# A two-layer hybrid decoder step: projections as seven block products for all tokens at once, with results passed through DRAM

## The chip, the cores and the metric

The kernel runs on one core of one Trainium2 chip. The metric is the device time of one execution in microseconds (us). The kernel before took 1739.54 to 1741.24 us in three runs, with a median of 1740.52 us. A profile of one more execution comes with it. In the profile PE is TensorE (PEld its weight loads), DVE is VectorE, ACT is ScalarE, POOL is GpSimd, and SP is SyncE, which issues all of this kernel's DMAs in one queue, in order.

## The reference, cut to what matters

One inference step of a decoder with two layers: 1024 prompt tokens, and 8 sample tokens (one each for 8 sequences with their own caches). The model is 1024 wide.

```python
for i in range(DEPTH):                      # 2
    hp, hs = rmsnorm(xp, norm_g[i]), rmsnorm(xs, norm_g[i])
    if i % 2 == 0:   # sliding-window attention, window 128, 32 heads of 64, 4 KV heads
        q, k, v, g = split(h @ w_in_attn)   # widths 2048, 256, 256, 2048
        o = softmax(q k^T / 8 + bias, masked, with a sink per head) v
    else:            # retention, 4 heads, 256 for q and k, 512 for v, chunks of 128
        q, k, v, g = split(h @ w_in_ret)    # widths 1024, 1024, 2048, 2048
        q, k = rotary(q), rotary(k) / 16
        o = groupnorm((q k^T * decay) v + (q R) * cross)
        R = gamma**128 * R + k_dec^T v
    x = x + (silu(g) * o) @ w_out           # 2048 x 1024
return rmsnorm(x), caches and states
```

All of it is float32. The largest part are the input projections: 4608 output features in layer 0 and 6144 in layer 1, each with an inner dimension of 1024, for 1032 tokens.

## The kernel before, in words

**A product in float32.** Every large operand is split in two: a high part rounded to fp32r (`whi`, `hh`, `yh`) and the rest (`wlo`, `hl`, `yl`). A product is three matmuls into one PSUM bank: high by high, high by low, low by high (lines 359 to 361). For a weight tile of 128x512 the split is one cast on ACT (line 175) and one subtraction, by turns on POOL and DVE (line 179).

**Two halves of the tokens.** The tokens are worked on in halves: half A is 512 prompt tokens and the 8 samples (520 columns, cut in 260 and 260), half B the other 512. The activations stand transposed, with features on the partitions. Each half goes through all weights of a layer, so each weight tile is loaded and split once for each half.

**The stream.** `Stream` holds the projection jobs in order. A job that produces 128 output features takes two weight tiles and 24 matmuls for each column block (`proj_job`), and evacuates the block from PSUM straight into what comes next: queries to their high and low parts (`q_jobs`), gates through silu (`g_jobs`, `rg_jobs`), rotary (`rot_jobs`). Values are made with the tokens on the PSUM partitions (`tok_job`). PSUM has four single banks for such jobs (`gps`, line 121). Output projections are jobs as well (`out_job`, `out1_job`): eight for each group of 512 inner features; each adds its product into the resident x.

**The order.** The order on PE is the order of the program text, written by hand; that of the other engines is planned from a model of their times. `spread(n, stages)` puts small pieces of attention or retention between n jobs of the stream. In layer 0 there are 64 attention pieces (two halves, eight groups of four heads, four blocks of 128 queries), each with scores (line 624), a softmax (lines 590 to 602), transposes (line 641) and values (line 663). In layer 1 there are 32 retention chunks (`ret_scores`, `ret_values`, `ret_turn`), and for each head one `ret_sample`, which reads and writes the sample states.

**Norms.** The norm of the next half or layer (`norm_stats`, `norm`) runs between attention pieces. In the first 30 us the input is taken in (`first_x`), in the projections' own order; its norm factor is applied after the product.

## Time and profile before

| | before |
|---|---|
| three runs, us | 1739.54, 1740.52, 1741.24 |
| profiled execution, its time and its span, us | 1736.38; 1734.6 |
| PE busy; PEld busy | 1697.7 us (98%); 1450.0 us (84%) |
| DVE; ACT; POOL busy | 60%; 48%; 41% of the span |
| DMA | 211.31 MB, 39.5% of 16 engines' time |
| mean granted TensorE clock | 0.994 |

The span is the time from the first to the last instruction. A matmul's shown duration contains the depth of its pipeline, and so the durations of matmuls that follow each other overlap: what one costs is read from the distance between two starts in the timeline, not from its duration. Groups of instructions are given by line, engine and operation, with tile names (out<-in), shape and count. The chain of waits is the sequence of work that ended last.

### The profile page before, as it was taken

Reading aid. Unit: us, or ns where it says so; the run is one execution under the profiler, and the core shown is the slowest. Engines: PE = TensorE matmul, PEld = TensorE weight load, DVE = VectorE, ACT = ScalarE, POOL = GpSimd, SP = SyncE. Lnnn points to the kernel's source line nnn. Section 1 sums busy time; section 2 is a strip of 40 time slices with the busy share of each in tenths; the row PEclk is TensorE's granted clock in tenths of the full one; section 3 lists DMA queues with packets and bytes.
Section 4 is the critical chain, followed back from the end, with each engine's and each line's share of the span. In section 5 each row is a group of like instructions: output and inputs, shape, how many; then the busy total and the mean of one; then the engine's idle time right before and its main releaser. Section 6 shows DMA issues by size and latency. Waiting matters only on the chain.

```text
span 1734.6 us, 29003 instructions
## 1 busy us (share of the span) xinstructions
PE 1697.7 (98%) x10550; PEld 1450.0 (84%) x10550; DVE 1045.5 (60%) x2142; ACT 841.1 (48%) x1960; POOL 713.2 (41%) x670
## 2 busy tenths in 40 slices
PE   9999999999999999999999999999999999999997
PEld 8989999988887777779788797897777889888887
DVE  6777676784576565773475545566555655445366
ACT  5566465555556464654344444344343433433344
POOL 3244344353344343444334235344353353433534
PEclk9999999999999999999999999999999999999998
DMA  5523333333253323223476445466463262322323
GB/s 153 142 62 91 123 105 104 89 108 91 85 172 90 85 75 92 80 86 106 120 244 192 143 152 188 128 195 206 129 217 111 85 194 73 98 86 81 102 69 121
DMA packets 124174, 211.31 MB, mean 122 GB/s; under 512 B 17128, under 2 KB 28000, under 8 KB 124032
## 3 DMA queue, kind: packets, MB, share of 16 engines
q1 hardware_dynamic: 124032, 209.47, 39.5%
q8 instruction: 83, 1.36, 0.3%
q14 instruction: 59, 0.48, 0.1%
HBM read 177.57 MB, written 33.91 MB: 122 GB/s over the span
## 4 chain that ended last, share of the span: by engine, by line
PE 81%; DVE 5%; DMA 3%; ACT 2%; POOL 2%; issue 1%; SPq 0%; POOLq 0%; ACTq 0%; DVEq 0%
PE gemm L359 12%; PE gemm L360 12%; PE gemm L361 12%; PE gemm L386 4%; PE gemm L387 3%; PE gemm L388 3%; PE o L663 3%; PE gemm L1063 3%; PE gemm L1062 3%; PE gemm L1064 3%; PE gemm L414 3%; PE gemm L416 3%; PE gemm L415 3%; PE S L624 3%; PE pt L641 1%
## 5 line engine op out<-in xcount | busy, mean ns | idle before, releaser
L179 POOL TENSOR_TENSOR wlo<-wraw,whi 128x512 fp32r<-128x512 f32 x236 | 311.7, 1321 | 555.6 <-ACT whi L175 524.0
L359 PE MATMUL gemm<-hh,whi 128*128 128x260 f32 (+1 forms) x1584 | 520.9, 329 | 0.0
L361 PE MATMUL gemm<-hh,wlo 128*128 128x260 f32 (+1 forms) x1584 | 506.2, 320 | 0.4 <-POOL wlo L179 0.4
L360 PE MATMUL gemm<-hl,whi 128*128 128x260 f32 (+1 forms) x1584 | 506.2, 320 | 0.0
L175 ACT CAST whi<-wraw 128x512 fp32r<-128x512 f32 x472 | 290.5, 617 | 442.9 <-PE gemm L360 136.5
L359 PEld LDWEIGHTS gemm<-hh,whi 128*128 128x128 f32 x1584 | 298.2, 188 | 45.0 <-issue 15.3
L361 PEld LDWEIGHTS gemm<-hh,wlo 128*128 128x128 f32 x1584 | 298.0, 188 | 23.3 <-POOL wlo L179 0.6
L360 PEld LDWEIGHTS gemm<-hl,whi 128*128 128x128 f32 x1584 | 298.5, 188 | 20.2 <-issue 0.5
L179 DVE TENSOR_TENSOR wlo<-wraw,whi 128x512 fp32r<-128x512 f32 x236 | 190.1, 806 | 161.6 <-ACT whi L175 159.5
L431 POOL TENSOR_TENSOR yl<-yf,yh 128x256 fp32r<-128x256 f32 x128 | 107.3, 847 | 96.7 <-ACT yh L430 96.3
L414 PE MATMUL gemm<-yh,whi 128*128 128x260 f32 (+1 forms) x384 | 126.9, 330 | 4.4 <-DVE xa L418 4.4
L386 PE MATMUL gemm<-whi,hh 128*128 128x512 f32 (+1 forms) x320 | 123.1, 385 | 2.9 <-DVE ra L748 2.8
L598 ACT ACTIVATE L<-L,nm 128x128 f32<-128x128 f32 x256 | 99.8, 391 | 52.2 <-DVE nm L593 51.8
L1062 PE MATMUL gemm<-yh,whi 128*128 128x260 f32 (+3 forms) x384 | 124.7, 325 | 0.0
L416 PE MATMUL gemm<-yh,wlo 128*128 128x260 f32 (+1 forms) x384 | 123.2, 321 | 0.0
L415 PE MATMUL gemm<-yl,whi 128*128 128x260 f32 (+1 forms) x384 | 123.0, 320 | 0.0
L1063 PE MATMUL gemm<-yl,whi 128*128 128x260 f32 (+3 forms) x384 | 122.8, 320 | 0.0
L1064 PE MATMUL gemm<-yh,wlo 128*128 128x260 f32 (+3 forms) x384 | 122.8, 320 | 0.0
L388 PE MATMUL gemm<-whi,hl 128*128 128x512 f32 (+1 forms) x320 | 120.0, 375 | 2.0 <-DVE hl L1099 1.8
L387 PE MATMUL gemm<-wlo,hh 128*128 128x512 f32 (+1 forms) x320 | 120.4, 376 | 0.0
L602 POOL TENSOR_TENSOR L<-L,rsum 128x512 f32<-128x512 f32 x64 | 76.4, 1193 | 79.3 <-DVE rsum L601 45.4
L414 PEld LDWEIGHTS gemm<-yh,whi 128*128 128x128 f32 x384 | 72.6, 189 | 15.2 <-ACT whi L175 4.8
(246 smaller groups left out, 3141.8 us busy)
## 6 DMA issues: line engine op xcount, KB each, us to landing
wraw<-in_w_in SPq DMA_DIRECT2D x264, 256.0 KB
wraw<-in_w_out SPq DMA_DIRECT2D x136, 256.0 KB
wraw<-in_w_v SPq DMA_DIRECT2D x72, 256.0 KB
Rsm<-in_state SPq DMA_DIRECT2D x64, 256.0 KB
out_ret_state_sample<-Rsm SPq DMA_DIRECT2D x64, 256.0 KB
vrow<-vdram SPq DMA_DIRECT2D x32, 256.0 KB
bias<-bdram SPq DMA_DIRECT2D x16, 256.0 KB
xdram<-xa SPq DMA_DIRECT2D x16, 256.0 KB
```

The lines of the kernel that those rows point to most:

```text
L175: act.copy(hi, raw)
L179: eng.tensor_tensor(out=lo, in0=raw, in1=r32(hi), op=ALU.subtract)
L359: pe.matmul(ps, a, hh[k][:, c0:c1], start=(k == 0), stop=False)
L360: pe.matmul(ps, a, hl[k][:, c0:c1], start=False, stop=False)
L361: pe.matmul(ps, b, hh[k][:, c0:c1], start=False, stop=(k == KT - 1))
L386: pe.matmul(ps, hh[k][:, cs], wh, start=(k == 0), stop=False)
L414: pe.matmul(ps, a, yh[:, k % 2, c0:c1], start=(k == 0), stop=False)
L415: pe.matmul(ps, a, yl[:, k % 2, c0:c1], start=False, stop=False)
L416: pe.matmul(ps, b, yh[:, k % 2, c0:c1], start=False, stop=(k == 3))
L1062: pe.matmul(ps, a, yh[:, k % 2, c0:c1], start=(k == 0), stop=False)
L1063: pe.matmul(ps, a, yl[:, k % 2, c0:c1], start=False, stop=False)
L1064: pe.matmul(ps, b, yh[:, k % 2, c0:c1], start=False, stop=(k == 3))
```

## The change

**Seven products a unit.** A unit is a pair of feature tiles (2 x 128 output features), the inner dimension in two halves of 512, and for each half of the tokens two blocks of columns: 256, and 256 with the samples (264; zeros stand in for the samples in half B). Plainly these are eight block products. The kernel after makes seven, with sums and differences of blocks (the form that is known as Winograd's): four weight blocks a, c, b, d give seven weight tiles (`mixed`), the four blocks of activations seven mixtures (`mixtures`). Each product is 12 matmuls (four inner tiles, three parts) for each half of the tokens; both halves are served from the same weight tile, `hi, lo`. Three results are put together outside PSUM. The seven mixtures of both halves, each with a high and a low part, stay in SBUF throughout a layer.

**Values** of both layers are made by such units as well, features on the partitions, and turned on PE afterwards (`v_unit`'s `turn`, `ret_scores`).

**PSUM.** A unit has two tiles of two banks (`a` and `y`); the next unit begins with their roles exchanged.

**Through DRAM.** Results of q, k, g and of all of layer 1 are stored (`spill`, or the end of `rot_unit`), and read back where they are needed (`load_gq`, `load_k`, `ret_load`); so are the gated branch outputs (`ydram`, `load_y`). Queries and keys are no longer split: scores are plain float32 with an inner dimension of 64, the two heads of a pair on partitions 0 to 63 and 64 to 127, their results in different banks.

**Output projections** come after the units as a stage of their own, with x read from DRAM and written back for every group of 512 inner features (`x_from`, `x_to`), both halves to one weight tile. Each x, each loaded branch output and each pair of rotary tables take one of three buffers (`flat`).

**Order.** In layer 0: values and keys of half A alone, of half B alone, 16 units of q and g with attention in between from the third on, then the output stage. In layer 1: gates of the first head for each half alone, the other units with retention between, the output stage.

```diff
-AHEAD = 2
+AHEAD = 1
+DEEP = 3
...
     def fetch(self, n):
         while self.todo and len(self.ready) < n:
-            self.ready.append(self.load(self.todo.pop(0)))
+            for w in self.todo[: 1 + DEEP]:
+                w.load()
+            self.ready.append(self.todo.pop(0).prep())
...
+    def big(name, dt=F32):
...
+        return ap_.tile([P, 2, 2 * QS], dt, name=name, tag="b", bufs=NBIG)
...
+    NBIG = 6
+    NHF = 3
...
+    def flat(name):
+        return ap_.tile([P, 2 * QS], F32, name=name, tag="hf", bufs=NHF)
...
+    def wtile():
+        return wp.tile([P, 512], F32, name="wraw", tag="wr", bufs=5)
...
+    def mixed(wa, wb):
...
+        def third():
+            minus(d["a"], d["b"], d["a"], vec)
+            d["t"] = wtile()
+            return wsplit(minus(d["t"], d["d"], d["a"], vec), vec)
...
+        return [
+            Weights(get(a=wa[0]), lambda: wsplit(d["a"], pool)),
+            Weights(get(c=wa[1]), lambda: wsplit(d["c"], pool)),
+            Weights(get(b=wb[0], d=wb[1]), third),
+            Weights(None, lambda: wsplit(d["a"], pool)),
+            Weights(None, lambda: wsplit(minus(d["b"], d["d"], d["b"], pool), vec)),
+            Weights(None, lambda: wsplit(d["d"], pool)),
+            Weights(None, lambda: wsplit(minus(d["c"], d["c"], d["t"], pool), vec)),
+        ]
...
+    def part(h, c, k, src, eng):
...
+        act.copy(hh, src)
+        eng.tensor_tensor(out=hl, in0=src, in1=r32(hh), op=ALU.subtract)
...
+    def mixtures(h, k, f):
...
+        a1, a2 = f[:, 0, 0:QS], f[:, 0, QS : 2 * QS]
+        b1, b2 = f[:, 1, 0:QT], f[:, 1, QS : 2 * QS]
+        part(h, 0, k, a1, pool)
+        part(h, 1, k, b1, vec)
+        part(h, 6, k, b2, vec)
+        vec.tensor_tensor(out=b2, in0=a2, in1=b2, op=ALU.add)
+        pool.tensor_tensor(out=a2, in0=a1, in1=a2, op=ALU.subtract)
+        vec.tensor_tensor(out=a1, in0=b2, in1=a1, op=ALU.subtract)
+        part(h, 2, k, a1, vec)
+        part(h, 3, k, b2, pool)
+        part(h, 4, k, a2, vec)
+        vec.tensor_tensor(out=b1, in0=b1, in1=a1[:, 0:QT], op=ALU.subtract)
+        part(h, 5, k, b1, pool)
...
+    def unit_job(wa, wb, done, halves=(0, 1)):
...
+            def product(ps, c, n, first):
+                hi, lo = stream.tile()
+                for i in range(nh):
+                    o = ps[:, i, :n]
+                    for k in range(4):
+                        hh, hl = [x[:, :n] for x in hcs[i][c][k]]
+                        wh, wl = hi[:, k * P : (k + 1) * P], lo[:, k * P : (k + 1) * P]
+                        pe.matmul(o, wh, hh, start=(first and k == 0), stop=False, skip_group_check=not first)
+                        pe.matmul(o, wh, hl, start=False, stop=False, skip_group_check=not first)
+                        pe.matmul(o, wl, hh, start=False, stop=(k == 3), skip_group_check=not first)
...
+            t = product(a, 0, QS, True)
+            x00 = ctile(0, nh)
+            act.copy(x00, aq)
+            yield t
+            t = product(y, 1, QT, True)
+            plus(x00, yq)
+            done(0, 0, x00, False)
+            yield t
+            t = product(a, 2, QS, False)
+            x10 = ctile(0, nh)
+            act.copy(x10, aq)
+            yield t
+            t = product(y, 3, QS, True)
+            x11 = ctile(1, nh)
+            act.copy(x11, yw)
+            yield t
+            t = product(a, 4, QS, False)
+            plus(x11, aw)
+            yield t
+            t = product(y, 5, QT, False)
+            plus(x10, yq)
+            done(1, 0, x10, False)
+            done(1, 1, x11, False)
+            yield t
+            t = product(a, 6, QS, False)
+            done(0, 1, aw, True)
+            yield t
...
+        for j in range(2):
+            for par in range(2):
+                r = slice(64 * par, 64 * par + 64)
+                pe.matmul(S[:, 2 * par + j, w0:256], q[r, j, cs], kk[r, (gb - 1) * P + w0 : (gb + 1) * P], start=True, stop=True)
...
+    def load_y(l, u):
...
+                f = flat("yf")[:, :T]
+                sp.dma_start(f, ydram[l][u][:, kt, h, 0:T])
...
+                act.copy(yh, f)
+                (pool if kt % 2 else vec).tensor_tensor(out=yl, in0=f, in1=r32(yh), op=ALU.subtract)
...
+    def rot_unit(f0, dr):
...
+            a = ctile(q, 2)
+            vec.tensor_tensor(out=a, in0=x1, in1=sin, op=ALU.mult)
...
+            vec.tensor_tensor(out=sin, in0=sin, in1=x2, op=ALU.mult)
+            pool.tensor_tensor(out=x2, in0=x2, in1=cos, op=ALU.mult)
+            vec.tensor_tensor(out=o1, in0=o1, in1=sin, op=ALU.subtract)
+            pool.tensor_tensor(out=x2, in0=x2, in1=a, op=ALU.add)
...
+    spread(outs[4], [stager(norm(0))] * 6)
+    spread(2, [stager(norm(1))] * 6)
+    stream.finish(2)
```

More of the change, by code (lines that the diff above doesn't have):

```diff
@@ L222, in norm_stats, with final_part @@
+    XF = {}
+    def final_part(c0, c1):
+        w = c1 - c0
+        xs = [XF[1, kt][:, c0:c1] for kt in range(KT)]
         s = None
         for kt in range(KT):
[L224 to L234 removed]
@@ L285, in final_part @@
[L285 to L291 removed]
+            b = flat("sqb")[:, :w]
             act.activation(b, xs[kt], AF.Square)
@@ L775, in rk_jobs @@
[L775 to L798 removed]
+    RS, RQ = {}, {}
```

1273 lines of the change are left out of this document (607 added, 666 removed).

## The prediction, made before the result was known

> **What bounds the kernel now.** I read the page's busy times and the chain of waits first, then the timeline of PE, then the grouped instructions.
>
> ```profile
> span 1734.6 us, 29003 instructions
> PE 1697.7 (98%) x10550; PEld 1450.0 (84%) x10550; DVE 1045.5 (60%) x2142; ACT 841.1 (48%) x1960; POOL 713.2 (41%) x670
> q1 hardware_dynamic: 124032, 209.47, 39.5%
> PE 81%; DVE 5%; DMA 3%; ACT 2%; POOL 2%; issue 1%; SPq 0%; POOLq 0%; ACTq 0%; DVEq 0%
> ```
>
> PE is the bound: 81% of the chain runs on it, and no other engine comes near its span. So PE's work counts first, and then every place where PE would begin to wait. A matmul's price is the distance between starts:
>
> ```profile
> 199.81 0.28 PE L359 MATMUL gemm<-hh,whi 128*128 128x260 f32 x1
> ...
> 202.57 0.28 PE L361 MATMUL gemm<-hh,wlo 128*128 128x260 f32 x1
> ...
> 999.77 0.40 PE L1062 MATMUL gemm<-yh,whi 128*128 128x512 f32 x1
> ...
> 1002.33 0.40 PE L1064 MATMUL gemm<-yh,wlo 128*128 128x512 f32 x1
> ...
> 1705.52 0.28 PE L1064 MATMUL gemm<-yh,wlo 128*128 128x256 f32 x1
> ...
> 1707.32 0.28 PE L1064 MATMUL gemm<-yh,wlo 128*128 128x256 f32 x1
> 1707.43 0.29 PE L1062 MATMUL gemm<-yh,whi 128*128 128x264 f32 x1
> ...
> 1710.26 0.28 PE L1064 MATMUL gemm<-yh,wlo 128*128 128x264 f32 x1
> ```
>
> The first and last of 24, 12, 16 and 24 in a row give 2.76/23 = 0.120 us for 260 columns, 2.56/11 = 0.233 for 512, 1.80/15 = 0.120 for 256, 2.83/23 = 0.123 for 264. The price follows the columns; cutting 512 in two costs nothing that shows, so the weight loads behind do not bind at these widths.
>
> **Products removed and added.** The counts of before:
>
> ```profile
> L359 PE MATMUL gemm<-hh,whi 128*128 128x260 f32 x1056 | 308.0, 292 | 0.0
> L359 PE MATMUL gemm<-hh,whi 128*128 128x512 f32 x528 | 212.9, 403 | 0.0
> L386 PE MATMUL gemm<-whi,hh 128*128 128x512 f32 x256 | 103.5, 404 | 2.9 <-DVE ra L748 2.8
> L386 PE MATMUL gemm<-whi,hh 128*128 128x256 f32 x64 | 19.6, 307 | 0.0
> L391 PE MATMUL vsp<-wlo,hs 128*40 128x512 f32 x32 | 12.6, 394 | 0.0
> ```
>
> Lines 360, 361, 387 and 388 have the same counts as 359 and 386, line 390 those of 391. Removed: 3168 x 0.120 + (1584 + 768 + 64) x 0.233 + 192 x 0.120 = 380 + 563 + 23, with some 2 us for 16 narrow sample products 968 us. Added: layer 0 has 18 units' worth (values and keys split by halves), layer 1 has 24. Each is 5 products of 24 matmuls at 264 columns and 2 at 256: 120 x 0.123 + 48 x 0.120 = 20.5 us. 42 units are 862 us. PE saves **106 us**, 11% instead of one eighth because of the zero columns. The output projections have as many columns as before.
>
> **PE work that comes in.** Scores change from eight split matmuls to four plain ones with an inner dimension of 64; values and their weights of attention are as they were.
>
> ```profile
> 202.69 0.60 PE L641 MATMUL pt<-cst,L 128*128 128x128 f32 x4
> 203.05 0.37 PE L359 MATMUL gemm<-hh,whi 128*128 128x260 f32 x1
> 226.60 1.01 PE o L663 x8
> 219.64 0.96 PE S L624 x8
> 307.67 1.10 PE rps L211 x2
> ```
>
> A plain matmul shows as two records, and `rps`, one of 512 columns, takes 1.10 us: 4 x 0.233 and the pipeline's depth, so four passes. Eight records of `o` are four plain matmuls of 256 columns; one after the other they would take 16 x 0.120 = 1.9 us. They take 1.01 us: two column halves of the array run side by side. For two row halves no row stands here: from 0.96 us (side by side, no change) to 1.9 us, or 0 to +61 us over 64 pieces. I take 0 by the row of `o`, nearest in kind, and add 0.25 us of a change of mode on either side, 16 us in all (before and after the eight records of `o` the neighbours stand so much further apart than 0.120). Turning values on PE: 128 + 18 transposes more, at 0.36/4 = 0.09 us, with the samples' small ones 15 us. Together **+31 us**.
>
> In a sentence that the sum doesn't use: the Trainium skill, TensorEngine Tiling (Array Packing), Gotcha 1: PSUM Pressure, says that row tiles can't reach the same PSUM bank at once; the code sends the two heads' scores to different banks, so that by it too the 61 us would stay away, and without that placing they would be paid; no run here shows it.
>
> **Work on the other engines.** Prices:
>
> ```profile
> L179 POOL TENSOR_TENSOR wlo<-wraw,whi 128x512 fp32r<-128x512 f32 x236 | 311.7, 1321 | 555.6 <-ACT whi L175 524.0
> L179 DVE TENSOR_TENSOR wlo<-wraw,whi 128x512 fp32r<-128x512 f32 x236 | 190.1, 806 | 161.6 <-ACT whi L175 159.5
> L175 ACT CAST whi<-wraw 128x512 fp32r<-128x512 f32 x472 | 290.5, 617 | 442.9 <-PE gemm L360 136.5 <-issue 85.0 <-PE gemm L388 58.5
> L1066 DVE TENSOR_TENSOR xa<-xa,gemm 128x512 f32<-128x512 f32 x32 | 21.9, 684 | 16.9 <-PE gemm L1064 16.5
> L647 ACT COPY ptp<-pt 128x512 f32<-128x512 f32 x56 | 32.3, 577 | 23.7 <-DVE ptc L643 19.9 <-DVE nm L593 3.6
> L558 DVE TENSOR_TENSOR qe<-qf,qe 64x260 fp32r<-64x260 f32 x32 | 16.6, 518 | 7.2 <-ACT qe L557 6.0
> L749 POOL TENSOR_TENSOR rf<-rf,ra 128x512 f32<-128x512 f32 x16 | 23.5, 1492 | 12.1 <-DVE ra L748 12.0
> 50.00:350.00 300.00, 292.10 (x2440) 272.77 (x2439) 216.52 (x506) 173.17 (x501) 122.94 (x121) 1.00 0.35 99
> ```
>
> A unit's weights take 7 casts on ACT (4.3 us), 5 DVE operations (4.0) and 6 on POOL (7.9); its results 4 copies on ACT (2.3) and 3 additions on DVE (2.1). That is 6.6, 6.1 and 7.9 us beside 20.5 us of PE, before attention. DVE is busy 72% from 50 to 350 us, with as many attention pieces to a us of PE as after; I expect the same share there, and no engine becomes the bound over a whole stage. So I cost this at nothing in the middle of the stages. Its cover is one product, 24 x 0.123 = 2.95 us, in which each PSUM tile must be emptied; where the cover is short it is a rival below.
>
> **Where PE waits anew.** The *head*: each of the four pairs of x blocks of a half needs four subtractions and three sums of 264 columns on DVE (7 x 0.52), two scalings and two sums of squares of 528 columns (4 x 0.7 by line 1066), 6.4 us; the first unit needs the last pair. Before, PE's first product came at 6.25 us:
>
> ```profile
> 6.25 0.56 PE L386 MATMUL gemm<-whi,hh 128*128 128x256 f32 x1
> 6.25:24.00 17.75, 15.39 (x108) 14.41 (x107) 16.42 (x33) 11.15 (x20) 8.73 (x6) 0.90 0.53 181
> 257.67 2.61 DMA sqb<-in_x
> 1184.51 4.94 DMA hf<-xdram
> 366.96 0.36 PE L414 MATMUL gemm<-yh,whi 128*128 128x260 f32 x1 [2.95 <-DVE xa L418]
> ```
>
> Now half A's mixtures end at 7 + 26 = 33 us (the first x lands near 7) and half B's, with the weights of the first two units between (2 x 5), near 70; values and keys of half B, 20.5 us, follow: 90 us, where the PE content is 6 + 41 + 2 = 49. That is up to 40 us; if ACT and POOL take their part in time and the scalings run at half, 15. I take +22, as before lost some 8 here itself. The *layer change* has the same work without squares (two halves, 5 us a pair, 20 us each) beside 22 us of output products and 20 us of gates: between +5 and +30, I take +12. In the eight *half-size units* 1.5 us of PE stands against one weight split of 0.6 + 1.3: 0 to +15, I take +5.
>
> The *output stages*: x and the branch outputs go through three buffers. An x is loaded, added and stored: at 2.61 us a transfer 2.6 + 0.7 + 2.6 = 5.9 us, a branch tile 2.6 + 0.6 + 1.3 = 4.5; for a group 16 x 5.9 + 8 x 4.5 = 130, over three buffers 43 us, and PE has 8 x (24 x 0.120 + 12 x 0.233) = 45 us. It just fits, and breaks at 4.94 us a transfer: 16 x 10.6 + 8 x 6.8 = 224, or 75 us. Retention and attention cover four of six groups. 0 to +55; I take +10. SP holds these stores behind the additions they wait for, and weight loads queue behind them; three tiles of lead (8.9 us) cover one such wait. The *rotary* units: tables are fetched through the same buffers, and PSUM is free only after them: 8 units, 0 to 3 us each; +8.
>
> New waits: **+57 us** (bounds 15 and 155). What could be below nothing: before's own waits, such as the 2.95 us at 366.96, where a norm held DVE, go with the stage that had them; that is the fast rival.
>
> The trace grants 0.90 of the clock from 6.25 to 24 us. The Trainium skill, TensorE: Matmul & The Clock Gate, Part 1: The HAM clock gate, has the clock halve after an idle window of 3.4 us and come back after as much of sustained work. By it the head and the layer change would cost some five returns of 1.7 us more, 8 us on the sum; the rows of before show dips, not such a price, and the sum leaves it out.
>
> **Sum.** 1734.6 - 106 + 31 + 57 = 1716.6 us of span. The profiled execution was 1.8 us above its span, and the median of the runs 4 us above that: 1722 us.
>
> **Rivals.**
> *Waits stay where they were* (faster). The planner puts the mixtures where DVE is free, and the transfers where SP is: of the 57 us nothing is left, 1722 - 57 = 1665 us. For it: POOL is idle 59% and ACT 52%. Against it: the head, where nothing else is there to do.
> *The two PSUM tiles are too few* (slower). Before, four single banks took turns; now a unit's next product but one needs its tile back, within 2.95 us, with DVE and ACT holding softmax or rotary work in their queues. One wait like the one at 366.96 in every second unit is 21 x 2.95 = 62 us: 1784 us. It decides the sign once the average is above 18 us, or 0.06 us for each of 294 products. For it: DVE at 72%; against it: four evacuations of 0.6 us in 20.5 us.
> *Scores one after the other* (slower): +61, 1783 us.
> *Transfers at 4.94 us everywhere*: 30 to 45 us more in uncovered output groups and rotary units, 1757 us. Traffic rises from 211 to about 320 MB (results 44 out and 46 back, branch outputs 34, x 72 more, weights 71 instead of 124): 39.5% becomes about 60%.
> *The saving isn't there*: columns or passes would have to cost more than in the rows above; 1740 or more, small.
>
> **How the numbers follow.** Forecast 0.37 (its own range 1700 to 1745), stay 0.23, two tiles 0.22, scores 0.07, transfers 0.10, no saving 0.01. A measurement here tells 0.2%, 3.5 us. Of the forecast 0.30 lies below 1737, 0.04 within 3.5 us of the median, 0.03 above; of the transfers 0.01, 0.02, 0.07. Faster 0.23 + 0.30 + 0.01 = 0.54, same 0.06, slower 0.40. The range reaches to the fast rival's side with its bounds (-25) and past the slow ones: 1640 to 1805.
>
> **What would show it.** Distances of 0.123 us between products, and about 862 us for them; scores of 0.96 or 1.9 us; PE's first stretch full only after 70 us or before 50; waits of PE named after DVE at the layer change; products waiting for ACT copies or DVE sums in the units; DVE sums waiting for x transfers in the output groups. I am wrong if the waits in the middle of the stages are larger than those at their ends.

## The result and the profile after

| | before | after |
|---|---|---|
| median of four runs, us | 1740.03 | 2109.82 |
| range, us | 1738.22 to 1741.24 | 2106.89 to 2119.58 |
| span of the profiled execution, us | 1734.6 | 2105.2 |
| mean granted TensorE clock | 0.994 | 0.914 |

The kernel after takes 1.214 times as long (95% interval 1.209 to 1.218). The forecast was 1722 us, with a range up to 1805 us. The page of after, in the lines that answer to those of before, and three rows of its DMA view:

```profile
span 2105.2 us, 33195 instructions
...
PE 1734.9 (82%) x12072; PEld 1548.8 (74%) x12072; DVE 1173.3 (56%) x2047; ACT 826.3 (39%) x1889; POOL 868.8 (41%) x737
...
q1 hardware_dynamic: 243776, 330.94, 50.3%
...
xdram<-xa SPq DMA_DIRECT2D x56, 260.0 KB, 3.1
...
xa<-xdram SPq DMA_DIRECT2D x48, 260.0 KB, 3.0
...
yf<-ydram SPq DMA_DIRECT2D x32, 260.0 KB, 4.2
```

PE stood idle for 37 us before (1734.6 - 1697.7) and stands idle for 370 us now, 333 us more. It is also busy for 37 us more, though it has fewer columns to work on; 333 and 37 together are the whole difference of 370.6 us between the spans. Where the idle time lies is told by busy time in windows. The columns are the window, its length, busy time and instructions of PE, PEld, DVE, ACT and POOL, the granted clock, the share of DMA time, GB/s. First before, where the stages of the two halves overlap: the head, and three windows up to 1600 us. Then after: head, units of layer 0, its output stage, layer change, units of layer 1, its output stage.

```profile
0.00:100.00 100.00, 92.54 (x695) 87.83 (x696) 71.15 (x157) 56.55 (x138) 32.16 (x33) 0.97 0.48 137
100.00:960.00 860.00, 849.92 (x5686) 728.38 (x5685) 548.28 (x1160) 470.79 (x1228) 363.83 (x356) 1.00 0.37 111
960.00:1010.00 50.00, 50.00 (x243) 40.66 (x242) 26.56 (x54) 19.52 (x37) 15.38 (x13) 1.00 0.40 121
1010.00:1600.00 590.00, 583.68 (x3201) 485.63 (x3200) 324.63 (x617) 241.09 (x453) 244.52 (x214) 1.00 0.45 140
```

```profile
0.00:105.00 105.00, 62.27 (x317) 53.79 (x318) 84.84 (x141) 54.25 (x125) 67.57 (x73) 0.72 0.42 121
105.00:620.00 515.00, 476.77 (x3724) 418.59 (x3724) 317.90 (x610) 255.26 (x718) 266.64 (x216) 0.96 0.40 125
620.00:900.00 280.00, 230.84 (x1537) 190.72 (x1535) 137.98 (x273) 96.42 (x270) 80.12 (x81) 0.94 0.63 197
900.00:1010.00 110.00, 68.19 (x309) 57.24 (x310) 78.17 (x131) 41.28 (x99) 63.24 (x55) 0.78 0.35 109
1010.00:1780.00 770.00, 648.11 (x4685) 609.51 (x4684) 401.11 (x624) 285.19 (x511) 318.74 (x250) 0.93 0.50 158
1780.00:2105.00 325.00, 248.72 (x1509) 218.99 (x1507) 153.30 (x269) 93.89 (x169) 72.48 (x65) 0.89 0.66 208
```

Length less PE's busy time gives the idle time of after: 43, 38, 49, 42, 122 and 76 us. The largest part is in layer 1, where DVE, ACT and POOL are busy for 52%, 37% and 41% of the window. None of them is near its limit, and yet PE waits. For what, is told by the waits (total us, times, longest). A row of PEld is the wait of a weight load, a row of PE that of the matmul itself; the two overlap and are not added.

```profile
PEld vtp L946 <- issue: 143.3, 31, 9.5
...
PE vtp L946 <- DVE ktl L937: 65.6, 14, 8.0
PE vtp L946 <- issue: 58.9, 15, 8.3
...
PEld gemm L521 <- issue: 42.6, 21, 9.5
...
PE pt L735 <- POOL L L687: 28.0, 12, 5.5
...
PE gemm L521 <- DVE xa L526: 26.7, 8, 6.2
...
PE gemm L521 <- DVE xa L529: 23.1, 4, 9.1
...
PE gemm L424 <- DVE cq L430: 13.1, 6, 8.0
...
PE gemm L424 <- DVE cq L846: 12.4, 3, 4.9
...
PE gemm L424 <- ACT cq L451: 7.2, 3, 3.9
...
PE gemm L424 <- ACT cq L439: 4.6, 3, 2.2
```

143 us by the weight loads, and 139 by the matmuls themselves, lie in front of the transposes of the values (`vtp`), one of the small additions of the prediction (15 us for all of them). One such place in the timeline, all engines, with the rows between left out:

```profile
1231.98 0.38 PE L927 MATMUL skt<-cst,qk 128*128 128x128 f32 x2
...
1236.48 0.58 ACT L439 COPY cq<-gemm 128x512 f32<-128x512 f32 x1 [7.62 <-DMA rq<-cq]
...
1238.51 0.47 ACT L935 ACTIVATE kth<-skt,cst 128x256 fp32r<-128x256 f32 x1
...
1240.13 0.47 DVE L937 SCALAR_TENSOR_TENSOR ktl<-skt,cst,kth 128x256 fp32r<-128x256 f32 x1
...
1240.70 1.08 PE L946 MATMUL vtp<-cst,v 128*128 128x128 f32 x4 [8.34 <-issue]
...
1242.22 0.41 PE L424 MATMUL gemm<-h01h,whi 128*128 128x256 f32 x1
...
1242.86 0.41 PE L424 MATMUL gemm<-h01h,whi 128*128 128x256 f32 x1
...
1243.43 0.78 ACT L895 ACTIVATE on<-ro,gr 128x512 f32<-128x512 f32 x1 [1.02 <-DVE gr L890]
...
1245.34 0.28 PE L424 MATMUL gemm<-h11h,whi 128*128 128x256 f32 x1
...
1245.69 0.28 PE L424 MATMUL gemm<-h11h,whi 128*128 128x256 f32 x1
```

The small PSUM pool (`wps`) has two banks. `ro` of the chunk before holds one until its group norm has read it, at 1243.43. `skt` holds the other until `ktl` has read it, at 1240.13 plus 0.47. The transposes stand right behind `skt` in PE's order and need a bank of this pool as well. So PE, which had nothing to do with keys or norms at that moment, waited 8.34 us for the whole chain on DVE and ACT, in which ACT itself had stood 7.62 us before a copy whose buffer an earlier store (`rq<-cq`) still held. And behind the wait the products run slowly: the three distances between starts from 1242.22 to 1242.86 are 0.213 us each, the three from 1245.34 to 1245.69 are 0.117 each, for the same 256 columns. The wait is paid a second time in the clock. The Trainium skill, TensorE: Matmul & The Clock Gate, Part 1, HAM oscillation, describes such a pattern for waits on DMA: a wait of more than some 3.4 us halves the clock, and the next burst starts cold. Here the trace agrees in the size, with 0.213 against 0.117 us, though not behind every wait: after one of 3.62 us in front of the transposes at 1369.96, the products run 0.12 us apart almost at once.

The numbers of waits by stage and of lost clock in some of the expectations below were summed from the distances between PE's starts: a distance of about twice the price of its columns counts as lost clock, anything else above the price by 0.15 us as a wait. By that sum the kernel before has 64 us of waits and 23 of lost clock, the kernel after 482 and 104. Short transitions, such as those between plain and fp32r matmuls, are in both kernels' waits. The sums are rough: with other bounds for "about twice" the same two traces give 27 to 49 us of lost clock before and 115 to 145 after.

### The profile page after: what moved, and what is told of

Read it like the earlier page. It is cut to its first block, busy times and chain, and to the rows that moved or that the text cites. A ratio compares the mean times of both kernels' runs of the same rounds, so it can differ in the third digit from the quotient of the medians.

```text
span 2105.2 us, 33195 instructions
## 1 busy us (share of the span) xinstructions
PE 1734.9 (82%) x12072; PEld 1548.8 (74%) x12072; DVE 1173.3 (56%) x2047; ACT 826.3 (39%) x1889; POOL 868.8 (41%) x737
## 5 line engine op out<-in xcount | busy, mean ns | idle before, releaser
L521 PE MATMUL gemm<-yh,whi 128*128 128x260 f32 (+2 forms) x800 | 273.0, 341 | 55.7 <-DVE xa L526 26.7
L523 PE MATMUL gemm<-yh,wlo 128*128 128x260 f32 (+2 forms) x800 | 262.9, 329 | 0.0
L522 PE MATMUL gemm<-yl,whi 128*128 128x260 f32 (+2 forms) x800 | 262.8, 328 | 0.0
L521 PEld LDWEIGHTS gemm<-yh,whi 128*128 128x128 f32 x800 | 162.4, 203 | 79.1 <-issue 42.6
L430 DVE TENSOR_TENSOR cq<-cq,gemm 128x512 f32<-128x512 f32 (+1 forms) x138 | 88.6, 643 | 150.1 <-PE gemm L426 123.6
L523 PEld LDWEIGHTS gemm<-yh,wlo 128*128 128x128 f32 x800 | 160.9, 201 | 11.2
L522 PEld LDWEIGHTS gemm<-yl,whi 128*128 128x128 f32 x800 | 162.1, 203 | 9.5
L230 POOL TENSOR_TENSOR wraw<-wraw 128x512 f32<-128x512 f32 x92 | 136.5, 1488 | 50.7 <-DVE wraw L230 26.4
L687 POOL TENSOR_TENSOR L<-L,rsum 128x512 f32<-128x512 f32 x64 | 74.0, 1157 | 148.8 <-DVE rsum L686 70.2
L946 PEld LDWEIGHTS vtp<-cst,v 128*128 128x128 f32 x128 | 18.3, 179 | 145.6 <-issue 143.3
L230 DVE TENSOR_TENSOR wraw<-wraw 128x512 f32<-128x512 f32 x92 | 87.7, 954 | 39.3 <-POOL wlo L202 28.7
L717 PE MATMUL S<-kk,q 64*128 64x256 f32 (+1 forms) x512 | 70.1, 392 | 2.6 <-DVE L L726 2.6
```

The source lines that it names most:

```text
L230: eng.tensor_tensor(out=out, in0=x, in1=y, op=ALU.subtract)
L430: vec.tensor_tensor(out=x, in0=x, in1=ps, op=ALU.add)
L521: pe.matmul(ps, a, yh[:, c0:c1], start=(k == 0), stop=False)
L522: pe.matmul(ps, a, yl[:, c0:c1], start=False, stop=False)
L523: pe.matmul(ps, b, yh[:, c0:c1], start=False, stop=(k == 3))
L687: pool.tensor_tensor(out=L, in0=L, in1=rs[:, :, None].to_broadcast([n, nh, P]), op=ALU.mult)
```

## The experiments

All times are medians of the comparison with the kernel before on the same chip, which stood at 1738 to 1740 us. "Less" is against the 2110 us of the kernel after. The planner orders the engines beside PE anew for each version, so every edit, above all one that leaves work out, also changes what stands before what there; for some runs the share of moved instructions is given.

**The value transposes in a piece of their own.**

```diff
+        CH["s"] = [sh, sl, kth, ktl, None, None, qh, ql]
+
+    def ret_v(u, gc):
+        d = RQ[u, gc // 2]
+        cs = slice(gc % 2 * P, gc % 2 * P + P)
         vt = wps.tile([P, 4, P], F32, name="vtp", tag="w")
...
-        CH["s"] = (sh, sl, kth, ktl, vh, vl, qh, ql)
+        CH["s"][4:6] = vh, vl
...
-        return [first, nothing, second]
+        def middle():
+            if j < 32:
+                ret_v(*divmod(j, 8))
+
+        return [first, middle, second]
```

> One edit on the changed kernel: the four transposes of a chunk's values leave the piece that also makes its scores and become the piece between, some products later. Theory A (one PSUM buffer too few in every chunk): scores and transposes of one piece need two buffers of the pool of two, while the chunk before still holds one until its group norm is done; PE stands in front of the value transposes 31 times for 143 us together, and half of these waits are long enough to be followed by a stretch at half clock. Then the wait in front of the value transposes falls below 30 us, the granted clock rises from 0.91 to about 0.95, and the time falls by 120 to 200 us, to 1910 to 1990 us. Theory B (DVE and ACT are the bound of layer 1 and the place is chance): the wait moves to the next piece that needs them, and the time stays above 2060 us.

Measured: 2009 us, 100 less, between the two theories and nearer to A. The wait in front of the value transposes falls from 143.3 to 39.6 us by the weight loads, where A had less than 30, and the granted clock of the whole run rises from 0.914 to 0.924 only, where A had 0.95. The windows of its layer 1:

```profile
1010.00:1690.00 680.00, 617.90 (x4605) 581.30 (x4604) 396.16 (x609) 272.85 (x494) 314.08 (x244) 0.96 0.56 175
1690.00:2005.00 315.00, 256.20 (x1540) 224.08 (x1539) 158.18 (x281) 98.30 (x177) 74.15 (x68) 0.90 0.69 217
```

In these windows idle time is 121 us (62 and 59), against 198. But at 1010 us this run was already ahead: the matmul that starts at 1010.2 us in the kernel after starts at 1002.8 here, before PE's order differs. From that matmul to the end, in both, idle time falls from 198 to 125 us and PE's busy time for the same work from 897 to 880 us: 73 us of waiting, and 16 us that go with the clock (0.93 to 0.96 in the units); the rest of the difference between the two spans lies ahead of it. Nothing was taken from any engine. What changed is the place in PE's order and, by the planner, that of some 4% of the instructions of DVE and ACT.

**Is the lost clock a price of its own?** Two runs. The first put fillers into a free quarter of the scores' bank:

```diff
+        for _ in range(16):
+            pe.matmul(w[:, 3 * P :], ones, ones, start=True, stop=True)
         vt = wps.tile([P, 4, P], F32, name="vtp", tag="w")
```

> One edit on the changed kernel: 16 matmuls of ones, 128 columns each, are put into the unused quarter of the scores' bank, in front of the value transposes where PE waits (31 waits, 143 us). They compute nothing that is used. Each takes four passes of 128 columns, 0.23 us, so 3.7 us in all, less than the mean wait of 4.6 us. Theory A1 (an idle PE has its clock halved, and this costs time of its own behind the wait): the wait is filled, the clock stays up, the transposes start as late as before, and the time falls by 20 to 50 us. Theory A2 (the low clock in the profile's rows follows from something else, or costs nothing): the time stays within 10 us of 2110 us, or rises by up to 60 us where the fillers outlast the wait.

Measured: 2231 us, 122 more, outside both. A row of its waits, and its group of fillers (busy us, mean ns, idle before), say why:

```profile
PEld skt L945 <- DVE ktl L937: 150.2, 32, 9.9
```

```profile
L945 PE MATMUL skt<-ones 128*128 128x128 f32 x1024 | 172.7, 347 | 142.5 <-DVE ktl L937 142.5
```

The fillers wrote to a tile that `ktl` still had to read, and so they waited themselves, as long as the transposes had, and ran behind the wait: 32 x 16 x 0.23 = 118 us. The run tells nothing of the clock. It does show that the wait is for `ktl`.

The second put 12 fillers into free columns of a tile of the units, in the same place:

```diff
             def product(ps, c, n, first):
+                idle[0] = y if ps is a else a
...
+        for _ in range(12 if idle[0] is not None else 0):
+            pe.matmul(idle[0][:, 0, 384:512], ones, ones, start=True, stop=True)
         vt = wps.tile([P, 4, P], F32, name="vtp", tag="w")
```

> The filled wait again, without the fault of the first try, whose fillers waited for the same reader of the scores' bank: 12 matmuls of ones (128 columns, 0.23 us each, 2.8 us) go into the columns that the unit's products leave free in the tile that isn't being evacuated, in front of the value transposes of the 24 chunks of the unit stage of layer 1. They compute nothing that is used. Theory A1 (a PE that stands idle loses clock behind the wait, at a price of its own): the transposes start as late as before, the fillers lie inside the waits (3.0 to 8.6 us in the trace), and the time falls by 10 to 40 us. Theory A2 (no such price): the time stays within 8 us of 2110 us. If the fillers wait for something themselves, it rises by up to 67 us.

Measured: 2088 us, 22 less (the fillers destroy sums that the units keep in that bank, so the results are not the reference's; the other work is the same). Its window of the units of layer 1:

```profile
1010.00:1760.00 750.00, 698.95 (x5303) 661.52 (x5303) 402.10 (x625) 284.25 (x509) 315.90 (x248) 0.97 0.52 163
```

A1: PE does more (300 matmuls, 12 in each of 25 places), the other engines do the same work in nearly the same order (7 of 1889 instructions of ACT and 12 of 2047 of DVE have moved), the granted clock of the stage is 0.97 instead of 0.93, and the kernel is faster. Counted from the same matmul as above, PE's busy time without the fillers is 884 us instead of 897. So 13 of the 22 us are seen as faster matmuls, near the 16 of the transposes' run; the rest is waiting that became shorter, and the run does not say why.

**Sixteen places for x.**

```diff
-            xa = flat("xa")[:, : real(h)]
+            xa = htile(h, 4 + ft // 4, ft // 2 % 2, "hl"[ft % 2], [P, TW], F32, "xa")[:, : real(h)]
```

> One edit on the changed kernel: in the output stages each x takes one of sixteen places of mixtures that are no longer read, instead of one of the three buffers that branch outputs use as well. Theory A (the three buffers are too few: x waits for the store of an earlier one, DVE's sum for x, PE for the sum): waits of PE in front of the output products (42.6 us by its weight loads, 26.7 and 23.1 us by its products) fall to less than half, and the time falls by 40 to 100 us. Theory B (the transfers themselves are too slow beside 50% of DMA time, or DVE comes too late for other reasons): the time falls by less than 20 us, and DVE's sums still wait for x.

Measured: 2046 us, 64 less: A. Waits and the window of the output stage of layer 0:

```profile
PE gemm L521 <- DVE xa L529: 7.7, 4, 3.6
...
PE gemm L521 <- DVE xa L526: 2.2, 1, 2.2
```

```profile
620.00:880.00 260.00, 241.75 (x1594) 199.79 (x1593) 149.86 (x299) 103.12 (x286) 83.22 (x84) 0.96 0.71 225
```

The waits of PE for the sums fall from 49.8 to 9.9 us. DMA is busier in this window than in that of after (71% against 63%), so the rate of the transfers was not the limit; the three buffers were.

**Six of seven mixtures left out.**

```diff
         part(h, 0, k, a1, pool)
-        part(h, 1, k, b1, vec)
...
-        part(h, 5, k, b1, pool)
+        for c in range(1, 7):
+            H[h][c][k] = H[h][0][k]
```

> The changed kernel with six of the seven mixtures of the activations left out: all seven products of a unit use the first mixture (the results are then not those of the reference); PE's work is the same. Of each block pair's seven casts on ACT, seven differences on DVE and POOL and four sums, one cast and one difference stay. Theory A (head and layer change are bound by the making of the mixtures, far above the 34 us that the prediction gave them): PE's first 105 us and the 110 us around the layer change shrink together by 60 to 110 us. Theory B (they were priced about right; the loss lies elsewhere): the time falls by 15 to 40 us. In both the rest of the time stays as it is.

Measured: 2051 us, 58 less, just short of A. PE's idle time in the first 78 us is 22 us, as the row shows, against 43 in the 105 us of the head of after.

```profile
0.00:78.00 78.00, 56.15 (x334) 49.65 (x335) 53.19 (x85) 38.36 (x79) 44.87 (x50) 0.85 0.57 166
```

**Attention one slot later.**

```diff
-            own.append(lambda: att_turn(i - 1))
+            own.append(lambda: att_turn(i - 2))
...
-            own.append(lambda: att_values(i - 2))
+            own.append(lambda: att_values(i - 3))
```

> One edit on the changed kernel: the transposes and the values of an attention piece come one slot later behind its scores (two slots and three instead of one and two); the three buffers of logits then are all in use. Theory A (in the units of layer 0 PE waits because the softmax, which passes DVE, ACT and POOL in turn, is not done one slot later): the waits of PE and of its weight loads in front of the transposed logits (28.0 and 36.9 us) fall below a third, and the time falls by 25 to 70 us. Theory B (PE waits for DVE in layer 0 wherever it needs it): the waits move to the transposed logits' readers and to the products' sums, and the time changes by less than 15 us either way.

Measured: 2094 us, 16 less, at the border of B. The wait that was aimed at nearly goes (28.0 to 3.6 us by the matmuls), as A had it, but the time follows only in part; another wait, 4.5 us in the kernel after, takes some of its place. The planner moved more here than in the other single edits that leave nothing out (11% of the instructions of DVE and of ACT, 16% of POOL's):

```profile
PE pt L735 <- DVE y L760: 8.8, 5, 3.0
...
PE pt L735 <- POOL L L687: 3.6, 1, 3.6
```

**The attention's work beside PE left out**, after and before (logits, softmax and the copies of the transposed logits).

```diff
-            pe.transpose(pt[:, e, :], L[:, e, :], ident)
-        ptc = lp.tile([P, 4, P], F32, name="ptc", tag="ptc", bufs=1)
...
+            pe.transpose(pt[:, e, :], ident, ident)
+        half = cst[:, P : 3 * P].rearrange("p (e t) -> p e t", e=2)
+        ptc, ptp = half, None if first else half
```

> The changed kernel with the attention's work between scores and values left out on DVE, ACT and POOL (mask, bias, softmax, the two copies of the transposed logits; the transposes and the values read constants, so the results are not those of the reference). PE's work and the transfers are the same. Theory A (in the changed kernel the pieces of attention are a second place where PE waits for the other engines, some 77 us of waits and 22 us of lost clock in the stretch from 105 to 620 us, and part of 66 us in the output stage of layer 0): the time falls by 60 to 120 us. Theory B (there PE waits for the units' own evacuations and weights): by less than 25 us.

> The same left out in the kernel before (mask, bias, softmax and the copies of the transposed logits; transposes and values read constants; the results are not those of the reference), as the other half of that comparison. Both theories: PE is the bound there and its waits over the whole span are small, so the time falls by 5 to 35 us. Were it to fall by as much as in the changed kernel, attention would not be what tells the two apart.

Measured: 2062 us, 48 less, between the theories; before, 1722 us, 0.991 of its time (0.989 to 0.993), 16 us less. So the same work costs PE 16 us in the one kernel and 48 in the other. In the window from 105 us PE's idle time is 8.4 instead of 38 us:

```profile
105.00:590.00 485.00, 476.60 (x3831) 423.75 (x3830) 143.11 (x254) 141.83 (x253) 188.99 (x128) 0.99 0.44 134
```

**The retention chunks' work beside PE left out** (splits, state, group norm).

```diff
-        sh, sl, kth, ktl, vh, vl, qh, ql = CH["s"]
...
+        vh = vl = CH["c"]
+        kth = ktl = vh[:, 0:256]
+        sh = sl = vh[:, 0:P]
+        qh = ql = kth.rearrange("p (a b) -> p a b", a=2)
```

> The changed kernel with the retention chunks' work on DVE, ACT and POOL left out (decay and splits of scores, keys, queries, values and state, the running state, the group norm; the products of a chunk and its transposes read constants, so the results are not those of the reference). PE's work and the transfers are the same. Theory A (PE waits in the chunks for these engines, 143 us in front of the value transposes and some 50 us of lost clock and other waits beside them): the time falls by 150 to 230 us, more than the 100 us that another place for the transposes gave. Theory B (the 100 us are all that the chunks cost): by 85 to 115 us.

Measured: 1973 us, 137 less, between the theories. The place of the transposes alone gave 100, with all of this work still done.

**The order of the scores.**

```diff
-        for j in range(2):
-            for par in range(2):
+        for par in range(2):
+            for j in range(2):
```

> One edit on the changed kernel: the four scores matmuls of an attention piece run in the order of their partitions (both of rows 0 to 63, then both of rows 64 to 127), so that only one pair of neighbours works on different rows of the array, instead of two. Theory A (different rows and different banks run side by side): a piece's scores take 1.5 passes' worth more than half as long again, some 0.5 us for each of 64 pieces, and the time rises by 0 to 35 us, as PE is bound there or waits anyway. Theory B (the rows take turns): the same durations in either order.

Measured: 2109 us, no change, and the same durations (here no instruction beside PE moved). The scores of after, then of this run, each with the next instruction on PE:

```profile
301.62 1.13 PE L717 MATMUL S<-kk,q 64*128 64x256 f32 x8
302.68 0.66 PE L735 MATMUL pt<-cst,L 128*128 128x128 f32 x4
```

```profile
309.35 1.14 PE L717 MATMUL S<-kk,q 64*128 64x256 f32 x8
310.42 0.39 PE L424 MATMUL gemm<-h00h,whi 128*128 128x264 f32 x1
```

1.06 and 1.07 us from the first start to the next instruction. The price is near the 0.96 us that the forecast took, but it does not hang on neighbours being on different rows. The single records say what it is. A plain matmul shows as two records, and in all 56 pieces with 256 columns the eight records stand in four pairs: the two of a pair start 7 ns apart in the kernel after and 13 ns in this run (medians), and a pair 0.216 us behind the one before, in both. In this run the first two matmuls are on the same rows. So, by the order of the program, a pair is the two records of one matmul, which run side by side where it fills only 64 rows: 4 x 0.216 us, and 0.2 us for the change of form. The two records of `rps`, which fills the array, start 0.43 to 0.52 us apart for 512 columns. The records of `o` in the kernel before, 64 columns of the array, stand in pairs too, 0.216 us from one to the next.

**The PSUM tiles of the units.**

```diff
-            aw, yw = a[:, :nh, :QS], y[:, :nh, :QS]
-            aq, yq = a[:, :nh, :QT], y[:, :nh, :QT]
+            aw = yw = cst[:, None, 0:QS].to_broadcast([P, nh, QS])
+            aq = yq = cst[:, None, 0:QT].to_broadcast([P, nh, QT])
```

> The changed kernel with the units' results not read from PSUM: every copy and every sum that empties a unit's tile reads a constant in its place, with the same form and at the same point of its engine's order (the results are not those of the reference). PE then never waits for a tile of the units. Theory A (the forecast's rival: two PSUM tiles are too few, one wait of 2.95 us in every second unit and more): the time falls by 60 us or more. Theory B (the four evacuations of a unit are mostly in time, and the waits named after them, some 37 us by PE's products, are the whole price): by 25 to 55 us. Theory C (these waits only move to the splits and the retention behind): by less than 20 us.

Measured: 2165 us, 55 more, outside all three. The units' products no longer wait for `cq`, but the splits come late instead, the wait of the value transposes grows (139 to 161 us by the matmuls), and the sums take longer. The group of sums, after and then in this run, and the largest wait of the units' products in this run:

```profile
L430 DVE TENSOR_TENSOR cq<-cq,gemm 128x512 f32<-128x512 f32 (+1 forms) x138 | 88.6, 643 | 150.1 <-PE gemm L426 123.6 <-issue 17.8 <-ACT gsm L998 4.5
```

```profile
L430 DVE TENSOR_TENSOR cq<-cq,cst 128x512 f32<-128x512 f32 (+1 forms) x138 | 117.6, 866 | 60.3 <-ACT cq L439 34.9 <-ACT cq L447 17.1 <-ACT cq L451 7.8
```

```profile
PE gemm L426 <- DVE wlo L202: 33.5, 11, 9.9
```

The replacement was not free of cost. The group mixes shapes; for 128x512 alone the means are 684 and 939 ns. The single sums of this run say where that comes from: 31 of 76 had no POOL instruction beside them and took 689 ns on average, 30 had one beside a part of them and took 1089, 15 had POOL busy all along and took 1157. In the kernel after, with one operand in PSUM, the same three means are 686, 678 and 684. The planner also put 23% of DVE's and 39% of ACT's instructions in another order. So the run does not price the rival, and does not refute it; what stands for it are the waits named after `cq`, 37 us in the four rows above.

**Edits that leave the results as they are, together.**

> Two edits on the changed kernel together: the value transposes in a piece of their own (alone: 2009 us, 100 us less) and sixteen places for x (alone: 2046 us, 64 us less). Theory A (two separate places of waiting): the gains add up, 1930 to 1960 us. Theory B (both give way to the same bound, the transfers or DVE): above 1975 us.

> All three edits on the changed kernel that leave the results as they are: value transposes in a piece of their own, sixteen places for x, transposes and values of attention one slot later (alone 100, 64 and 16 us less; the first two together 155). Theory A (separate places): 1930 to 1950 us. Theory B (what is won in attention is lost again in the output stage or to the clock): 1950 to 1965 us. Neither reaches the 1740 us of the kernel before.

> The three edits that leave the results as they are (1933 us), and in the rotary units the last product copied out of PSUM by ACT at once, where before DVE read it there behind the tables. Theory A (the products that wait for the rotary sums, some 24 us, get their PSUM tile back earlier): 10 to 30 us less, 1903 to 1923 us. Theory B (ACT is late there as well): 1925 to 1945 us.

Measured: 1955, 1933 and 1918 us, each within its theory A. The last one copies the rotary units' last product out at once:

```diff
         def done(f, q, x, psum):
+            if psum:
+                t = ctile(q, 2)
+                act.copy(t, x)
+                x, psum = t, False
             got[f, q] = x
```

It is the fastest version with the change that leaves nothing out, and still takes 1.103 times as long as the kernel before (1.101 to 1.106).

**Closing the books.** Everything named taken away at once, then retention's work as well, then the rotary tables' transfers, or instead the preparation of six of seven weight tiles (one split for all seven products). The edits of the last two:

```diff
-                sp.dma_start(t, I["rope"][i][:, :, span(q)])
...
-            Weights(get(c=wa[1]), lambda: wsplit(d["c"], pool)),
+            Weights(get(c=wa[1]), lambda: d["w"]),
```

> Every place of waiting that was named is taken away at once: value transposes in a piece of their own, sixteen places for x, six of seven mixtures left out, and the attention's work between scores and values left out on DVE, ACT and POOL (the last two leave out part of the computation, as in their own runs). PE's work is that of the changed kernel. Theory A (the products' saving is there and waits ate it): the single gains of 155, 58 and 60 to 120 us add up, 1780 to 1840 us, and the rest above PE's own work is the retention's and the clock's. Theory B (PE's work itself is larger than the durations say): nothing below 1900 us.

> All that was named taken away at once (1840 us), and the retention chunks' work on DVE, ACT and POOL left out as well. What is left beside PE's work is the units' own evacuations and weights, rotary, transfers, the sample states and what remains of head and layer change. Theory A (the products' saving is there; without its covers PE's work is some 75 to 110 us less than that of the kernel before): the time falls below that kernel's 1740 us, to 1690 to 1745 us. Theory B (the rest is in the units themselves): 1770 to 1840 us.

> The kernel before this one, with the rotary tables not loaded either (constants take their place; the results are not those of the reference; the same additions and products on DVE and POOL). Theory A (in the rotary units PSUM is free late since their tables come late, through three buffers): 10 to 35 us less than the run before it. Theory B (DVE's and POOL's own work there is what is late): within 8 us of it.

> What was left at 1774 us (all named places and the retention's other work taken away), and of a unit's weights only the first tile is split on ACT and POOL; all seven products use it, and the sums and differences of weight blocks are left out (the results are not those of the reference). PE's work and the loads are the same. Theory A (products wait for the splits in the units, 17.7 us by PE's weight loads for ACT's casts and a part of 39.6 us that is put to no engine): 30 to 60 us less, 1715 to 1745 us. Theory B (the weights are ready in time, and the rest stands at head, layer change, output stages, rotary and in the clock): 1755 to 1780 us.

Measured: 1840, 1774, 1781 and 1735 us. The first is at the edge of its theory A. The second is theory B: the saving did not show yet once retention was gone. The third is B too, so the tables' transfers are not what is late there. The fourth is A: the preparation of weights was a further 38 us. Its page:

```profile
span 1732.8 us, 29167 instructions
...
PE 1635.1 (94%) x12072; PEld 1475.8 (85%) x12072; DVE 482.1 (28%) x857; ACT 369.7 (21%) x649; POOL 292.5 (17%) x243
```

With the same 12072 records of PE as the kernel after, PE is busy for 1635 us, 63 less than in the kernel before, at a clock of 0.972. This version takes as long as the kernel before (0.998 of it, 0.996 to 1.000), with DVE relieved of 691 of its 1173 us, ACT of 457 of 826 and POOL of 576 of 869.

## Why the prediction was wrong

**PE's columns: right.** A product of 24 matmuls of 264 columns in after, first and last:

```profile
1139.95 0.28 PE L424 MATMUL gemm<-h02h,whi 128*128 128x264 f32 x1
...
1142.75 0.28 PE L426 MATMUL gemm<-h12h,wlo 128*128 128x264 f32 x1
```

2.80/23 = 0.122 us; the forecast had 0.123. PE's whole work was to be 75 us less (106 less 31). Where few waits are left, in the version at 1735 us, it is 63 less by busy time. The lower clock there, 0.022 of 1733 us, hides up to 38 us more, so an estimate is 63 to 101. The saving exists, and it is covered with waiting.

**Scores: right in size, not in reason.** 1.06 us a piece against 0.96 is 6 us in 64, within 0 to 61; the reason given was two matmuls on two row halves side by side. The run that changes their order speaks against it: it is the two records of one matmul that run together. The reading of `o` as two column halves side by side is open to the same correction.

**The step that failed** is "So I cost this at nothing in the middle of the stages". The prediction compared shares: 6.6, 6.1 and 7.9 us on ACT, DVE and POOL beside 20.5 us of PE, and DVE at 72% as before. In the window from 105 to 620 us DVE has only 62%, and PE waits more. What had to be compared is the lead at each place where PE takes a buffer: how long the chain on DVE, ACT and POOL is that must end first, and how many products stand between. The transposes of values were costed by their duration and not by the PSUM bank that they take: 100 us came back by another place for them. The other places of the middle: attention's work beside PE costs 48 instead of 16 us, the preparation of the weights 38 us (measured with the others gone). The prediction's own condition, that it is wrong if waits in the middle of the stages are larger than those at their ends, came true against head and layer change: the two stages of units hold 160 us of idle time, those two 85. The output stages hold 125 more; whoever counts them as ends has 210 there.

**The waits that were named were too small.** Their bounds together, 15 and 155 us, are 20 and 164 by the prediction's own terms; PE stands idle for 333 us more. Head and layer change together have 85 us of idle time, where before 7 stood in the first 100 us and 16 in all the 1500 us that follow, against +22 and +12 forecast (bounds up to 40 and 30); 58 us came back without six of the seven mixtures. Output stages: +10 forecast, 64 came back by sixteen places for x. There the working had 43 us of buffer time against 45 of PE and called it "just fits". With the transfers that the rows of after show (3.0 and 3.1 us for an x in and out, 4.2 for a branch output, where the working had 2.61) the same sum is 16 x 6.8 + 8 x 6.1 = 158, or 53 us over three buffers: it does not fit. Rotary: +8 forecast; 15 us came back by one copy (1933 to 1918).

**The clock left out of the sum.** The prediction named 8 us for five returns of 1.7 us and left them out. Behind the wait at 1240.70 the return cost about that: some 16 distances are 0.096 us too long, 1.5 us. The number of returns was wrong: by the rough sums the lost clock is 104 us after against 23 before. Rows of before couldn't price it, since before hardly waits; two runs of after do, with 16 and 13 us of PE's busy time for the transposes alone.

**The rivals.** "Two PSUM tiles too few" was the nearest in kind, one PE wait for one late reader, but at the wrong pool: the waits for the units' own tiles are 37 us by the four rows named after `cq` (62 forecast; no run prices them), those for the two small banks beside them 139. "Transfers at 4.94 us everywhere" did not come: 3.0 to 4.2 us by the rows shown, traffic 331 MB and 50% where 320 and 60% were forecast. But the shorter transfers were enough to break the output groups, as said. "Scores one after the other" did not come.

**What stays open.** In the kernel at 1735 us PE still stands idle for 98 us where before it was 37. The runs do not separate what is left of head, layer change, output stages and clock.

## What to carry to other kernels

When work is cut from an engine that is 98% busy, the other engines' slack by share is no cover, as here: go through its order and ask at each buffer it takes which chain must end first and how much of its own work stands between. Two uses of a small pool in one piece, with a third still held, put that whole chain on the critical path; moving one use some products later gave back 100 us without changing any work. And long waits on PE (31 here, 4.6 us on average) are to be counted with the clock that they cost: 16 us beside 73 here.

## What was not expected of the hardware

Extra matmuls made a kernel faster: 300 of them, put into waits of PE, gave 22 us, with the granted clock of their stage at 0.97 instead of 0.93.

A sum on DVE of 128x512 takes longer when both operands lie in SBUF and POOL works beside it: 689 ns without POOL and 1157 ns with POOL busy all along, in the run on the PSUM tiles; with one operand in PSUM POOL makes no difference (686 and 684 ns). The kernel before has it too: the subtraction of a weight split on DVE (line 179) takes 688 ns alone and 1016 beside POOL. The prediction's 806 ns was the mean of both. The Trainium skill, GPSIMD Engine Reference, section 1, Specifications, has POOL share SBUF interfaces with VectorE and names instructions with two SBUF inputs as those that contend; the trace agrees, with 1157 against 689 ns.
